# Moving the second half of the first v from SyncE's DMA queue to GpSimd's, with another share of rows for each DMA engine

## Chip, cores, metric

One core of a Trainium2 chip. The metric is the device time of one execution in microseconds (us).

## The reference

```python
# attn_weights: (8, 12, 1024, 1024) float32, v: (8, 12, 1024, 64) float32
def reference(attn_weights, v):
    return np.einsum('bhqs,bhsd->bhqd', attn_weights, v).astype(np.float32)
```

It reads 403 MB of weights and 25 MB of v and writes 25 MB (the page has 427.82 MB read and 25.17 MB written). Nearly all of the time is the reading of the weights: the last of them land at 1031.2 of 1052.7 us.

Of the kernel before, what the change touches and what calls it, by code (L numbers as in the profile page):

```python
# [10 lines left out]
def kernel(  # L11
# [18 lines left out]
    nc = tc.nc  # L30
    fp32 = mybir.dt.float32
# [6 lines left out]
    P = 128  # L38
# [17 lines left out]
    NO = 8 + 2  # L56
# [3 lines left out]
    def slot(q):  # L60
# [7 lines left out]
    v_2 = v.rearrange("b h q d -> (b h) q d").rearrange(  # L68
        "(hq two four) (p r) d -> hq (four p) two (r d)", two=2, four=VH, p=VP
    )  # L70
# [11 lines left out]
    with tc.tile_critical(no_gpsimd_drain=True):  # L82
        sem = tc.alloc_semaphore
        sb = lambda name, shape, dt: nc.alloc_sbuf_tensor(name, shape, dt).ap()
# [4 lines left out]
        vr = sb("vr", [P, 2, VB, SB * D], bf16)  # L89
        vbf = sb("vbf", [P, SB, VH, D], bf16)  # L90
        ot = sb("ot", [P, GH, P], fp32)
        osb = sb("osb", [P, NO, 2 * G, D], fp32)

        v32 = osb[:, ds(NO - 2, 2)].rearrange("p n r d -> p (n r d)")
        bank = [nc.alloc_psum_tensor(f"bank{i}", [P, 512], fp32).ap() for i in range(8)]
        pt = [b.rearrange("p (k j) -> p k j", k=KW) for b in bank[:4]]
        po = bank[4:6]
# [2 lines left out]

        s_abf = [sem(f"s_abf{i}") for i in range(2)]
        s_second = {n: sem(f"s_second{n}") for n in range(HALVED, NU)}
        s_v0, s_v = sem("s_v0"), sem("s_v")
        s_osb = [sem(f"s_osb{i}") for i in range(2)]
        s_held, s_end = sem("s_held"), sem("s_end")

# [11 lines left out]
        s_memset, s_const, s_vr = sem("s_memset"), sem("s_const"), sem("s_vr")  # L118
# [184 lines left out]

        for h in range(2):
            nc.vector.memset(ot[:, :, ds(h * HP, HP)], 0.0).then_inc(s_ot[h])
        nc.vector.wait_ge(s_v0, 16 * 4)
        nc.vector.tensor_copy(out=vr.rearrange("p two b x -> p (two b x)"), in_=v32).then_inc(s_vr, 2)  # L307
        engine(True)
        engine(False)

# [1 line left out]
        pool = nc.gpsimd  # L312

        def load_attn(n):
            pieces = [(0, G)] if n < HALVED else [(0, GH), (GH, GH)]
            for g0, gn in pieces:
                pool.dma_start(  # L317
                    out=abf[n % 2][:, ds(g0, gn)].rearrange("p g s -> p (g s)"),
                    in_=attn_q[n // 2][:, ds((n % 2 * G + g0) * S, gn * S)],
                ).then_inc(s_abf[n % 2] if g0 == 0 else s_second[n], 16)  # L320
# [15 lines left out]
        def store_2(q):  # L336
            store(q, 2, pool, s_osb[q // 2 % 2] if q < HELD_FROM else s_held)

        load_attn(0)
        load_attn(1)  # L340
        pool.wait_ge(s_memset, 2)
        pool.affine_select(
            out=ident,
            in_=ident,
# [7 lines left out]
        for h in range(VH):  # L352
            pool.wait_ge(s_const, h + 1)
            pool.affine_select(  # L354
                out=spread[ds(h * VP, VP)],
                in_=spread[ds(h * VP, VP)],
# [6 lines left out]
        for n in range(NU - 2):  # L363
            q, i = n // 2, n % 2
# [10 lines left out]
        pool.drain()  # L375





        v32_2 = v32.rearrange("p (two x) -> p two x", two=2)
        for two, p0, pn in ((0, 0, P), (1, 0, 96), (1, 96, 22), (1, 118, 10)):
            nc.sync.dma_start(
                out=v32_2[ds(p0, pn), two], in_=v_2[0][ds(p0, pn), two]
            ).then_inc(s_v0, 16)
        nc.sync.sem_inc(s_free, 2)
        for n in range(-2, NU - 2):

            if n + 2 < HALVED:
                nc.sync.wait_ge(s_abf[n % 2], 16 * ((n + 2) // 2 + 1))  # L390
            else:
                nc.sync.wait_ge(s_second[n + 2], 16)
            nc.sync.sem_inc(s_half)  # L393
            if n >= 0 and n % 2 == 0:
                q = n // 2
                if q % 2 == 1 and q + 1 < NV:
                    nc.sync.wait_ge(s_v, 16 * ((q + 1) // 2))
                    nc.sync.sem_inc(s_vr, 2)
                if q % 2 == 1 and 1 < q <= HELD_FROM:
                    nc.sync.wait_ge(s_osb[(q - 3) // 2 % 2], 16 * ((q - 3) // 4 + 1))  # L400
                    nc.sync.sem_inc(s_free)
# [10 lines left out]
        for k in range(2):  # L412
            nc.sync.wait_ge(s_osb[k], 16 * (HELD_FROM // 4))
        nc.sync.wait_ge(s_held, 16 * (BY_SYNC - HELD_FROM) // 2)
        nc.sync.wait_ge(s_end, 16 * 5)


# [28 lines left out]
```

## The kernel before: what the change touches

The weights come in 48 loads of 8 MB (64 KB in each of 128 rows; GpSimd's queue casts them to bf16 on the way, 4 MB land: 128 packets of 32768 bytes for each load in the trace). Two buffers take them in turn, and load n+2 is issued when PE has transposed load n. The v of eight heads comes as 128 rows of two halves; later v's come by GpSimd's queue too, but the first one comes by SyncE's queue, in float32, into a part of the output buffer that is not needed yet, and VectorE casts it:

```python
v32 = osb[:, ds(NO - 2, 2)].rearrange("p n r d -> p (n r d)")
...
# VectorE
nc.vector.wait_ge(s_v0, 16 * 4)
nc.vector.tensor_copy(out=vr.rearrange("p two b x -> p (two b x)"), in_=v32).then_inc(s_vr, 2)
...
# GpSimd
load_attn(0)
load_attn(1)
...                                     # constants
for n in range(NU - 2):                 # NU = 48
    q, i = n // 2, n % 2
    if i == 0 and q % 2 == 1 and q + 1 < NV:
        ...                             # wait until the v before is used
        load_v((q + 1) // 2)
    pool.wait_ge(s_t[True], (n + 1) * PER_DVE)
    load_attn(n + 2)
    if i == 0 and q % 2 == 0 and 0 < q <= HELD_FROM:
        store_2(q - 2)                  # 2 MB of the output, single_packet=True
...
# SyncE
v32_2 = v32.rearrange("p (two x) -> p two x", two=2)
for two, p0, pn in ((0, 0, P), (1, 0, 96), (1, 96, 22), (1, 118, 10)):
    nc.sync.dma_start(
        out=v32_2[ds(p0, pn), two], in_=v_2[0][ds(p0, pn), two]
    ).then_inc(s_v0, 16)
```

The split 96, 22 and 10 of the second half was already a balance: the rows per engine that the prediction counts in the trace, 17 on ten, 16 on one and 14 on five, fit eight rows of the first half and six of the 96 on each engine, two of the 22 rows on 11 engines and one of the 10 rows on ten of these, so that five engines get fewer rows.

## Time and profile before

| | before |
|---|---|
| median of the first three runs | 1055.8 us (1054.4 to 1056.23) |
| span in the profile | 1052.7 us |
| DMA engines' mean busy share | 90% or more in 39 of 40 slices, 80% to 90% in the last |
| PE, VectorE, ScalarE busy | 70%, 37%, 38% |
| last weights landed | 1031.2 us |

The waits say the same from two sides (columns: who waited for whom, us in total, times, longest us); the first line is from the view of all engines, the second from SyncE's queue:

```profile
POOL abf L317 <- PE bank L130: 689.1, 35, 34.0
...
SPq L393 <- DMA abf<-in_attn_weights_dram: 1025.5, 48, 25.7
```

GpSimd waits for PE before it may issue a load, which looks like a PE bound. But SyncE, which does little else than wait for loads to land, waits 1025.5 of 1052.7 us for them: there is always a load under way.

Besides the views, this document uses the trace's packet records: start, duration, size and queue of each DMA packet. They do not name the DMA engine; the prediction tells how packets were chained by time. That an engine sends one packet after the other is taken from the records: with 0.03 us taken off the end of each packet (a weight packet starts 0.02 us before the one ahead of it ends), more than 16 packets are under way at no time from 3 to 1030 us before. The 16 completion marks of each load are taken to tell when each engine was done with it: in load 2 before, each of its 16 packets of 4 bytes starts within 0.02 us of the end of a weight packet, at 65.30 to 67.07 us, and the marks come at 65.58 to 67.36 us. A number given to an engine here is a place in the layout of the rows; no record shows it. "The landing of load 2" below is the last of its 16 marks; loads count from 0.

Two packets of 16 KB come by an instruction queue (q8). Before, they start at 45.99 us (0.94 us long) and 56.29 us (0.98 us), and the weight packets right behind them take 2.605 and 2.607 us instead of 2.432, so each sets the engine that carries it back by 1.1 us.

### The profile page before, as it was taken

What the parts mean: (1) busy time and instruction counts of PE and PEld (TensorE: products, weight loads), DVE (VectorE), ACT (ScalarE), POOL (GpSimd) and SP (SyncE); (2) the same over time, 40 slices, a digit from 0 to 9 for tenths busy, and PEclk for the clock granted to TensorE, in tenths of its full rate; (3) what the DMA queues carried; (4) which work ended last, traced back from release to release, by engine and by line L of the source; (5) the groups of instructions that cost most, each with busy time, mean ns of one, the idle gap of its engine ahead of it and who ended that gap; (6) DMA issues with size and microseconds to landing.
All of it is one profiled execution on the core that took longest, in us unless ns stands there. A gap on an engine that the chain in (4) does not pass through costs nothing.

```text
span 1052.7 us, 16283 instructions
## 1 busy us (share of the span) xinstructions
PE 733.0 (70%) x6920; PEld 687.1 (65%) x6920; DVE 388.2 (37%) x582; ACT 397.8 (38%) x485; POOL 45.1 (4%) x80
## 2 busy tenths in 40 slices
PE   0777687676687567667768657775766865875885
PEld 0767676566687567656668557765666865865875
DVE  0543344333353234333335324433333433532543
ACT  0443344433353334333335324433333533533543
POOL 1000000000000000000000000000000000000000
PEclk9989888898798888889879878888887987988998
DMA  9999999999999999999999999999999999999998
GB/s 236 223 219 216 212 252 219 219 218 247 232 212 252 215 219 258 218 219 228 241 214 215 259 218 218 259 219 213 247 220 219 218 209 228 218 206 224 211 217 341
DMA packets 14332, 240.20 MB, mean 228 GB/s; under 512 B 1269, under 2 KB 1781, under 8 KB 4725
## 3 DMA queue, kind: packets, MB, share of 16 engines
q0 software_dynamic: 12912, 233.84, 99.1%
q1 hardware_dynamic: 1413, 6.29, 1.5%
q8 instruction: 2, 0.03, 0.0%
q14 instruction: 5, 0.04, 0.0%
HBM read 427.82 MB, written 25.17 MB: 430 GB/s over the span
## 4 chain that ended last, share of the span: by engine, by line
DMA 77%; PE 21%; issue 1%; POOL 0%; DVE 0%; ACT 0%; POOLq 0%; SPq 0%
DMA abf<-in_attn_weights_dram 77%; PE bank L130 20%; PE bank L172 0%; PE bank L157 0%; POOL abf L317 0%; DVE osb L237 0%; ACT ot L266 0%; POOLq L441 0%; SPq L393 0%; SPq L82 0%
## 5 line engine op out<-in xcount | busy, mean ns | idle before, releaser
L130 PE MATMUL bank<-ident,abf 128*128 128x128 f32 x3072 | 449.1, 316 | 278.0 <-DMA abf<-in_attn_weights_dram 272.6
L130 PEld LDWEIGHTS bank<-ident,abf 128*128 128x128 f32 x3072 | 439.2, 214 | 291.3 <-DMA abf<-in_attn_weights_dram 284.7
L254 DVE COPY at<-bank 128x1024 bf16<-128x1024 bf16 x480 | 319.8, 689 | 466.0 <-PE bank L130 463.0
L254 ACT COPY at<-bank 128x1024 bf16<-128x1024 bf16 x288 | 288.8, 1012 | 429.9 <-PE bank L130 429.9
L172 PE MATMUL bank<-at,vbf 128*64 128x256 bf16 x3072 | 215.0, 278 | 0.0
L172 PEld LDWEIGHTS bank<-at,vbf 128*64 128x64 bf16 x3072 | 196.8, 108 | 13.4 <-DVE at L254 4.0
L266 ACT COPY ot<-bank 128x512 f32<-128x512 f32 x48 | 28.1, 586 | 181.0 <-PE bank L172 181.0
L266 DVE COPY ot<-bank 128x512 f32<-128x512 f32 x48 | 33.2, 692 | 151.4 <-PE bank L172 151.4
L157 PE MATMUL bank<-ident,ot 128*128 128x128 f32 x392 | 52.2, 276 | 33.0 <-DVE vbf L230 32.2
L157 PEld LDWEIGHTS bank<-ident,ot 128*128 128x128 f32 x392 | 43.4, 141 | 45.0 <-DVE vbf L230 44.0
L237 ACT COPY osb<-bank 128x512 f32<-128x512 f32 x97 | 52.2, 589 | 22.5 <-PE bank L157 22.5
L317 POOL DMA_DIRECT2D abf<-in_attn_weights_dram x50 | 27.3, 546 | 690.2 <-PE bank L130 689.1
L230 DVE CAST vbf<-bank 128x512 bf16<-128x512 f32 x48 | 30.9, 686 | 6.5 <-PE bank L145 6.5
L230 ACT CAST vbf<-bank 128x512 bf16<-128x512 f32 x48 | 25.8, 589 | 11.9 <-PE bank L145 11.9
L145 PE MATMUL bank<-vr,spread 32*128 32x512 bf16 x384 | 25.7, 377 | 0.0
L323 POOL DMA_DIRECT2D vr<-in_v_dram x11 | 7.8, 706 | 238.5 <-PE bank L145 238.5
L145 PEld LDWEIGHTS bank<-vr,spread 32*128 32x128 bf16 x384 | 10.0, 92 | 6.9
L307 DVE CAST vr<-osb 128x4096 bf16<-128x4096 f32 x1 | 2.3, 2294 | 28.3 <-DMA osb<-in_v_dram 28.3
L330 POOL DMA_DIRECT2D out_dram<-osb x10 | 7.2, 717 | 28.6 <-ACT osb L237 28.6
L254 ACT ACT_TABLE_LOAD x4 | 5.1, 1283 | 1.1 <-SPq L82 1.1
L354 POOL TENSOR_SCALAR_AFFINE_SELECT spread<-spread 32x512 bf16<-32x512 bf16 x4 | 2.5, 632 | 0.6
L237 DVE COPY osb<-bank 128x512 f32<-128x512 f32 x1 | 0.7, 693 | 3.1 <-PE bank L157 3.1
(8 smaller groups left out, 2.1 us busy)
## 6 DMA issues: line engine op xcount, KB each, us to landing
abf<-in_attn_weights_dram POOLq DMA_DIRECT2D x46, 4096.0 KB, 33.4
out_dram<-osb POOLq DMA_DIRECT2D x10, 2048.0 KB, 29.5
vr<-in_v_dram POOLq DMA_DIRECT2D x11, 1024.0 KB, 17.4
abf<-in_attn_weights_dram POOLq DMA_DIRECT2D x4, 2048.0 KB, 24.2
out_dram<-osb SPq DMA_DIRECT2D x1, 2048.0 KB, 13.7
osb<-in_v_dram SPq DMA_DIRECT2D x1, 1024.0 KB
out_dram<-osb SPq DMA_DIRECT2D x1, 1024.0 KB, 16.0
osb<-in_v_dram SPq DMA_DIRECT2D x1, 768.0 KB
```

Source lines behind the costliest of these rows:

```text
L130: last = pe.matmul(out=pt[g % 4][:, k], lhsT=words[:, k], rhs=ident, is_transpose=True, start=(k == 0), stop=(k == KW - 1),)
L145: last = pe.matmul(out=ps, lhsT=spread[rows, b], rhs=vr[rows, two, b], start=(b == 0), stop=(b == VB - 1),)
L157: last = pe.matmul(out=ps[:, ds(j * P, P)], lhsT=ot[:, j0 + j], rhs=ident, is_transpose=True, start=(j == 0), stop=(j == jn - 1),)
L172: last = pe.matmul(out=outs, lhsT=vbf[:, 2 * kw + par, h], rhs=at[:, ds(half * GH, GH), kw, ds(h * VP, VP), par], start=(n == 0), stop=(n ...
L230: copy(out=vbf[:, :, h], in_=ps.rearrange("p (k d) -> p k d", k=SB)).then_inc(s_vbf[e])
L237: return copy(out=rows.rearrange("p (half j) d -> p j half d", half=2)[:, ds(j0, jn)], in_=ps[:, ds(0, jn * P)].rearrange("p (j half d) -> ...
L254: ins = copy(out=at[:, g].rearrange("c k j two -> c (k j two)"), in_=bank[g % 4].bitcast(bf16),)
L266: copy(out=ot.rearrange("c j (h p) -> c h j p", h=VH)[:, ds(2 * e, 2)], in_=po[e].rearrange("c (h j p) -> c h j p", h=2, j=GH),).then_inc( ...
L317: pool.dma_start(out=abf[n % 2][:, ds(g0, gn)].rearrange("p g s -> p (g s)"), in_=attn_q[n // 2][:, ds((n % 2 * G + g0) * S, gn * S)],).th ...
L323: pool.dma_start(out=vr.rearrange("p two b x -> p two (b x)"), in_=v_2[iv]).then_inc(s_v, 16)
L330: eng.dma_start(out=out_2[q // 2] if fours == 2 else out_q[q], in_=at_slot if fours == 2 else at_slot[:, 0], **({"single_packet": True} if ...
L354: pool.affine_select(out=spread[ds(h * VP, VP)], in_=spread[ds(h * VP, VP)], compare_op=mybir.AluOpType.not_equal, fill=1.0, base=0, patte ...
```

## The change

Its intent, read from the diff: only the first half stays on SyncE's queue; the second goes straight into its bf16 place by GpSimd's queue, behind loads 0 and 1. Three tiny transfers into an unused tile stand around the rows; the author took them to be there to shift which engines the 42 rows leave out.

```diff
-        v32 = osb[:, ds(NO - 2, 2)].rearrange("p n r d -> p (n r d)")
+        v32 = osb[:, NO - 1].rearrange("p r d -> p (r d)")
+        unused = sb("unused", [13, 3, 16], fp32)
...
-        nc.vector.wait_ge(s_v0, 16 * 4)
-        nc.vector.tensor_copy(out=vr.rearrange("p two b x -> p (two b x)"), in_=v32).then_inc(s_vr, 2)
+        nc.vector.wait_ge(s_v0, 16)
+        nc.vector.tensor_copy(out=vr[:, 0].rearrange("p b x -> p (b x)"), in_=v32).then_inc(s_vr)
...
+        to, of = vr[:, 1].rearrange("p b x -> p (b x)"), v_2[0][:, 1]
+        def lead(i, k):
+            pool.dma_start(out=unused[0:k, i], in_=v_2[0][0:k, 0, 0:16]).then_inc(s_unused, 16)
+        def rows_of_v(p0, p1):
+            pool.dma_start(out=to[p0:p1], in_=of[p0:p1]).then_inc(s_v1, 16)
+        lead(0, 13)
+        rows_of_v(0, 42)
+        lead(1, 5)
+        rows_of_v(42, 122)
+        rows_of_v(122, 128)
+        lead(2, 10)
...
-        for two, p0, pn in ((0, 0, P), (1, 0, 96), (1, 96, 22), (1, 118, 10)):
-            nc.sync.dma_start(...).then_inc(s_v0, 16)
+        nc.sync.dma_start(out=v32, in_=v_2[0][:, 0]).then_inc(s_v0, 16)
...
+            if n == 0:
+                nc.sync.wait_ge(s_v1, 16 * 3)
+                nc.sync.sem_inc(s_vr)
...
+        nc.sync.wait_ge(s_unused, 16 * 3)
```

More of the change, by code (lines that the diff above doesn't have):

```diff
@@ L102 @@
         s_second = {n: sem(f"s_second{n}") for n in range(HALVED, NU)}
-        s_v0, s_v = sem("s_v0"), sem("s_v")
+        s_v0, s_v1, s_v, s_unused = sem("s_v0"), sem("s_v1"), sem("s_v"), sem("s_unused")
         s_osb = [sem(f"s_osb{i}") for i in range(2)]
@@ L375 @@
         pool.drain()
-        v32_2 = v32.rearrange("p (two x) -> p two x", two=2)
-        for two, p0, pn in ((0, 0, P), (1, 0, 96), (1, 96, 22), (1, 118, 10)):
-            nc.sync.dma_start(
-                out=v32_2[ds(p0, pn), two], in_=v_2[0][ds(p0, pn), two]
-            ).then_inc(s_v0, 16)
+        nc.sync.dma_start(out=v32, in_=v_2[0][:, 0]).then_inc(s_v0, 16)
         nc.sync.sem_inc(s_free, 2)
         for n in range(-2, NU - 2):
+            if n == 0:
+                nc.sync.wait_ge(s_v1, 16 * 3)
+                nc.sync.sem_inc(s_vr)
             if n + 2 < HALVED:
```

## The prediction

Step 2 shared the rows among the engines: two engines, called 11 and 12, get five rows of the second half (six before), the others eight or nine; "11 to 15" are the five with the fewest rows before.

> **What bounds the kernel now.** I read the page first, then the chain of waits, then the timeline of the first 60 us, then the trace's records of single DMA packets. The page, parts 2 to 4:
>
> ```profile
> DMA  9999999999999999999999999999999999999998
> ...
> q0 software_dynamic: 12912, 233.84, 99.1%
> q1 hardware_dynamic: 1413, 6.29, 1.5%
> q8 instruction: 2, 0.03, 0.0%
> ...
> DMA 77%; PE 21%; issue 1%; POOL 0%; DVE 0%; ACT 0%; POOLq 0%; SPq 0%
> ```
>
> The 16 DMA engines are full in every slice; GpSimd's queue (q0) alone takes 99.1% of their time, SyncE's (q1) 1.5%. The chain's 21% on PE is not a PE bound, as its pieces show (start us, length us, what):
>
> ```profile
> 2.16 45.86 DMA abf<-in_attn_weights_dram
> 48.07 8.03 PE bank L130 x64
> 56.10 0.29 issue
> 56.39 30.33 DMA abf<-in_attn_weights_dram
> ...
> 1001.34 29.87 DMA abf<-in_attn_weights_dram
> 1031.29 5.60 PE bank L130 x32
> ```
>
> A load is issued when its buffer is free, but its packets then stand behind those of the load before it, so the eight microseconds of PE lie beside that load's packets. The bound is a sum of packet times on each DMA engine, from the first packet to the landing of the last attention weights at about 1031.2 us. The 21.5 us from there to the end (1052.7) are transposes, products and the last stores, which the change does not touch.
>
> The start, which the change does touch, in the timeline:
>
> ```profile
> 0.96 1.91 SPq L383 DMA_DIRECT2D osb<-in_v_dram  x4
> 1.48 1.24 POOL L317 DMA_DIRECT2D abf<-in_attn_weights_dram  x2 [1.04 <-SPq L82]
> 28.63 3.69 PE L130 MATMUL bank<-ident,abf 128*128 128x128 f32 x16 [28.63 <-DMA abf<-in_attn_weights_dram]
> 30.87 2.29 DVE L307 CAST vr<-osb 128x4096 bf16<-128x4096 f32 x1 [28.31 <-DMA osb<-in_v_dram]
> 33.82 6.08 PE L130 MATMUL bank<-ident,abf 128*128 128x128 f32 x48 [1.51 <-DVE at L254]
> 40.20 0.57 POOL L317 DMA_DIRECT2D abf<-in_attn_weights_dram  x1 [33.98 <-PE bank L130]
> ```
>
> The reader is to see that DVE waits 28.31 us for the first v, that its cast then holds PE for 1.51 us, and that load 2 goes out at 40.20 us, still before load 1 has landed (PE starts on it at 48.07).
>
> The packet records give start, duration, size and queue of each packet, not its engine; but an engine sends one after the other, so I chained them by time. What they show: a row of attention weights (64 KB read, 32 KB written) is one packet of 2.43 us, one every 2.41 us; a row of v takes 0.322 us by SyncE's queue and 0.324 us by GpSimd's, which casts it, one every 0.305 us. SyncE's first packets start at 1.98 us (eight engines) or 2.67 to 2.92 us (the other eight), GpSimd's first ones at 5.6 to 6.3 us on 14 engines and at 7.66 us on two. Two engines carry one 16 KB packet each of the instruction queue q8, at 45.99 us (0.94 us) and 56.29 us (0.98 us). From 3 us to 1030 us the engines' idle time is about 0.02 us in each 20 us.
>
> [...] the packets per chain at the start fit 17 rows on ten engines, 16 on one, 14 on five (they sum to 256), which is what 128, 96, 22 and 10 rows give. [...]
>
> **The change, part by part.**
> 1. Removed: 128 row packets on SyncE's queue. Added: 128 row packets on GpSimd's, behind loads 0 and 1. Mean per engine: 8 x 0.305 = 2.44 us taken out and put back. Sum zero. The f32 staging shrinks by half, which frees no time.
> 2. Added: three transfers of 13, 5 and 10 rows of 64 bytes into an unused tile, one or two small packets per engine. My estimate is at most 0.1 us on an engine (the trace's 4-byte packets take 0.02 us). [...]
> 3. What the new split is for: before, the three lightest chains that started early land load 1 at 46.00 to 46.31 us and the full ones at 46.9 to 47.35; then the q8 packet and the slower packet beside it set one engine back by 1.1 us, to 47.77 us, the last. An engine with 3.4 rows fewer (3.4 x 0.305 = 1.04 us) just absorbs such a packet: 8.4 rows against 5. So if 11 and 12 are the two that carry q8, all end load 1 and the v rows at about 5.9 + 16 x 2.41 + 8.5 x 0.305 = 47.1 us (estimate), up to 47.4 with the spread, and the last one gains about 0.4 us.
> 4. What it costs: SyncE's 8 rows are over at about 5.0 to 5.6 us and GpSimd's queue starts at 5.6 to 6.3. Before, second-half rows filled that gap; now it is idle: about 0.3 us on 14 engines. The two that start at 7.66 us are worse: before they moved some five rows of v meanwhile; now they idle about 2 us and owe those rows. If they are 11 and 12, they end at 7.66 + 38.6 + 5 x 0.305 = 47.8 us, or 48.9 with a q8 packet; if among 13 to 15, at 48.7 us. That is +0.1 to +1.1 us against 47.77. Their packet counts (about 14) put them among 11 to 15.
> 5. Off the path: the cast of v halves (2.29 us to an estimated 1.15 us) and need no longer wait for 28 us; load 0 lands without rows of v between its packets, so PE starts earlier by about 1.5 us and load 2 goes out perhaps 4 to 5 us earlier. Its queue is not empty at 40.20 us anyway, so this gives at most the 0 to 0.3 us by which the first engine runs dry near 46 us. The second half of v is in place at about 48 us and is used one loop round later, past 80 us.
>
> And the start is not all kept: the spread of the loads' landings falls from 1.77 us to 1.27 at about 148 us, where the last packets before the first store take 2.9 to 3.3 us on the leading engines. After that 13 engines lie within 0.8 us, and two trail, to 1.69 and 2.02 us at the end. An imbalance at the start is worth about half its size at the end. Sum: -0.4 + 0.3 to +1.1, halved: about -0.2 to +0.4 us. With the mark that whoever chose 42 rows and five rows for two engines will have aimed at the trailing ones, I take -0.2 us: 1055.8 to 1055.6.
>
> **The rivals.**
> First, the trailing engines at the end are exactly 11 and 12, and the row less there (6 to 5), with the load moved to engines that lead, shortens the end by 0.3 to 1 us: 1054.8 to 1055.5. For it: the clean arithmetic of 3.4 rows. Against: the two late starters, which lose their filling.
> Second, the late starters become the last ones and stay so: +1 us, 1056.8. For it: the gap of 1.5 us in the first GpSimd packets; against: the evening out at 148 us, and that the late start may itself come from SyncE's rows, which take 0.45 to 0.61 us instead of 0.32 on those two engines just then.
> Third, the early end of load 0 shortens the whole by several us because PE waits for 28.63 us at the start. Against: PE is never the bound later, the queues are full; worth nothing.
> Fourth, more packets on GpSimd's queue delay its descriptors for later loads. Load 2 is the first issued after them, at over 35 us, and six issues of about 0.55 to 0.7 us each are long over: 0 us.
>
> **Range and chances.** All of these lie within 2 us, 0.2% of the time. The three runs before spread over 1.8 us (1054.4 to 1056.23)[...], so the range that should hold the time 8 times in 10 is 1054.0 to 1057.4 us. For 2% (21 us) about ten rows of weights per engine would have to vanish or be added: faster 0.005, within 2% 0.985, slower 0.01 (a queue stall that I don't see).
>
> **What would show each step.** q1's bytes fall by 1 MB; q0 has 128 more packets of 4096 bytes and a few of 64. The cast of v is about 1.1 us long and comes before 10 us; PE starts at about 27 us and load 2 is issued at about 35 us. GpSimd's first packets start at the same 5.6 to 7.7 us; if those two engines are no longer late, step 4 is too dark. The landings of the last load show who trails: a spread clearly under 2.0 us with an earlier last one says the rebalancing works; about 3 us says rival two. The last landing should stay within 1 us of 1031.2 us and the tail at 21.5 us. I would be wrong if the tail, the load period of 43.5 us for two loads, or the idle time between 60 and 1000 us changed.

## The result, and the profile after

| | before | changed |
|---|---|---|
| median of 6 runs each | 1054.72 us (1054.37 to 1056.23) | 1055.17 us (1054.93 to 1055.92) |
| ratio | | 1.0003, 95% interval 0.999 to 1.0015 |

A ratio here is the mean time of one kernel's runs over that of the other's runs of the same rounds, so it is not quite the ratio of the medians quoted.

The timeline of the start (start us, busy us, engine, line, what, and in brackets the idle time before it and who ended it; line numbers are one or more higher than before):

```profile
0.96 0.39 SPq L397 DMA_DIRECT2D osb<-in_v_dram  x1
...
5.78 1.23 DVE L308 CAST vr<-osb 128x2048 bf16<-128x2048 f32 x1 [3.21 <-DMA osb<-in_v_dram]
...
25.08 10.33 PE L131 MATMUL bank<-ident,abf 128*128 128x128 f32 x64 [25.08 <-DMA abf<-in_attn_weights_dram]
...
35.71 0.59 POOL L318 DMA_DIRECT2D abf<-in_attn_weights_dram  x1 [25.47 <-PE bank L131]
```

The cast takes 1.23 us and is over at 7 us instead of 33. PE starts at 25.08 instead of 28.63 us and is not held up, and load 2 is issued at 35.71 instead of 40.20 us. The queues in the page:

```profile
q0 software_dynamic: 13200, 234.36, 99.4%
q1 hardware_dynamic: 1248, 5.24, 1.3%
q8 instruction: 2, 0.03, 0.0%
```

1 MB has left q1; q0's share rises from 99.1% to 99.4%, q1's falls from 1.5% to 1.3%. The work has changed queues and has not become less. The chain's last part:

```profile
1002.95 28.42 DMA abf<-in_attn_weights_dram
...
1031.45 6.69 PE bank L131 x32
```

PE starts on the last weights at 1031.45 us, 0.16 later than before, although it started on the first ones 3.55 us earlier.

The packet records show where the 3.55 us went. In the table "mean" is the mean of the 16 completion marks, "last" the last of them, and "stretched" is the time that weight packets took above their usual 2.432 us in the stretch from 144 to 151 us, summed over the engines:

| us | before | changed |
|---|---|---|
| GpSimd's first weight packets | 5.62 to 7.67 | 5.03 to 5.37 |
| load 0, last | 28.58 | 25.03 |
| load 2, mean / last | 66.55 / 67.36 | 66.21 / 67.14 |
| load at 130 us, mean / last | 129.44 / 130.22 | 129.10 / 130.01 |
| stretched | 5.0 | 14.7 |
| load at 150 us, mean / last | 149.10 / 149.92 | 149.36 / 150.48 |
| last load, mean / last | 1029.89 / 1031.21 | 1030.02 / 1031.37 |

Load 0 is early because rows of v no longer stand between its packets. Before, they came one between two rows of weights: most of them started at 8.08 to 8.70, 10.81 to 11.43 and 13.54 us and so on, 2.73 us apart (2.41 + 0.32), the last at 27.43 us. In the changed kernel the rows come after load 1, at 43.75 to 47.18 us, and by load 2 nothing of the 3.55 us is left but a mean lead of 0.34 us. The last engine leads by 0.22 us only. At 145 us both are lost in a stretch of slow packets, on the last weight rows ahead of the first store. The sum closes: from load 2 to the end the mean lead of 0.34 us turned into a lag of 0.13, a loss of 0.47 us, and the weight packets after 67 us were over their usual time by 9.1 us in sum before and 16.3 us in the changed kernel, which is 0.45 us per engine.

### The profile page after: what moved, and what is told of

Same layout as the page of the kernel before. It is cut to its first block, busy times and chain, and to the rows that moved or that the text cites. A ratio compares the mean times of both kernels' runs of the same rounds, so it can differ in the third digit from the quotient of the medians.

```text
span 1052.8 us, 16286 instructions
## 1 busy us (share of the span) xinstructions
PE 738.6 (70%) x6920; PEld 693.1 (66%) x6920; DVE 387.9 (37%) x582; ACT 397.7 (38%) x485; POOL 49.1 (5%) x86
## 3 DMA queue, kind: packets, MB, share of 16 engines
q0 software_dynamic: 13200, 234.36, 99.4%
## 4 chain that ended last, share of the span: by engine, by line
DMA 77%; PE 21%; issue 1%; POOL 0%; DVE 0%; ACT 0%; SPq 0%; POOLq 0%
DMA abf<-in_attn_weights_dram 77%; PE bank L131 20%; PE bank L173 0%; PE bank L158 0%; POOL abf L318 0%; DVE osb L238 0%; ACT ot L267 0%; POOLq L457 0%; SPq L408 0%; SPq L82 0%
## 5 line engine op out<-in xcount | busy, mean ns | idle before, releaser
L131 PE MATMUL bank<-ident,abf 128*128 128x128 f32 x3072 | 454.7, 319 | 273.7 <-DMA abf<-in_attn_weights_dram 269.7
L131 PEld LDWEIGHTS bank<-ident,abf 128*128 128x128 f32 x3072 | 445.2, 214 | 286.5 <-DMA abf<-in_attn_weights_dram 281.8
```

The lines of the kernel that those rows point to most:

```text
L131: last = pe.matmul(out=pt[g % 4][:, k], lhsT=words[:, k], rhs=ident, is_transpose=True, start=(k == 0), stop=(k == KW - 1),)
```

## The experiments

Twelve runs were made: the two kernels unchanged, nine other versions, and one of these a second time. My theory A: the end is a sum of packet times on each engine, so moving v gives nothing, and the uneven shares of rows matter only for the engine that trails. Two things stood against the intent of the change and had to be tested: whether the two engines with five rows are those that carry the instruction packets, and whether a start lead survives at all.

All runs (last landings in us, from the traces; the median of the kernel before is that of the same session; stretched as above, for the last two kernels with later stores at 164 to 168 us; "no second half" was read from 142.9 us):

| run | load 2, last | stretched | last of all | median | before | ratio |
|---|---|---|---|---|---|---|
| before again | 69.05 | 9.8 | 1032.27 | 1055.70 | 1054.94 | 1.0005 |
| changed again | 67.31 | 14.3 | 1031.93 | 1055.70 | 1054.94 | 1.0008 |
| plain | 67.23 | 10.9 | 1031.41 | 1055.15 | 1054.94 | 1.0003 |
| split as before | 66.66 | 11.5 | 1032.20 | 1055.56 | 1054.94 | 1.0006 |
| no second half | 64.69 | 10.9 | 1028.97 | 1052.76 | 1055.50 | 0.9975 |
| second half twice | 69.55 | 9.7 | 1033.78 | 1057.76 | 1055.50 | 1.0022 |
| no small transfers | 67.23 | 11.0 | 1032.19 | 1055.72 | 1055.50 | 1.0002 |
| no single packets | 67.16 | 10.9 | 1031.60 | 1055.47 | 1055.50 | 1.0002 |
| one SyncE transfer | 67.53 | 3.3 | 1031.68 | 1055.36 (one look) | 1055.37 | none |
| stores later | 67.39 | 14.0 | 1031.49 | 1055.08 | 1055.37 | 0.9996 |
| split again | 66.77 | 10.2 | 1032.15 | 1055.46 | 1055.37 | 0.9999 |
| split, stores later | 66.60 | 10.1 | 1030.65 | 1054.85 | 1055.27 | 1.0000 |

The 95% intervals of the ratios reach about 0.0015 to each side; only those of "no second half" (0.9962 to 0.9989) and "second half twice" (1.0009 to 1.0036) leave 1 out. So differences of under a microsecond between the other versions are read from the traces, one or two each, and not from the times.

### Both kernels once more

No edit.

> The kernel before, unchanged, for a second trace of it. Every theory expects the same time (ratio 1.000 within 0.1%). What it tells: how much the packet records repeat. If the landings of load 2 come again with the last at 67.1 to 67.4 us and 1.8 us of spread, and the two 16 KB instruction packets near 46 and 56 us hit the same kind of engine, the start is set by the program; if the one-off stretching of the packets near 145 to 150 us (5 us summed over the engines in the first trace) comes out otherwise, that part is chance.

> The changed kernel, unchanged. Ratio to the kernel before 0.999 to 1.001. Theory A (the shares of GpSimd's partial copies go from the lowest engine up, 42 rows as 3 on each of 14 engines, so the relief of 42 rows went to two engines that carry no instruction packet): the trace again has two engines that start load 2 near 45.6 us and one at 47.5 us with the first instruction packet, and the last landing of load 2 at about 67.1 us. Rival B [...]: in another execution the two relieved engines may be the ones with the instruction packets, and the last landing of load 2 falls to about 66.5 us. The stretching near 145 to 150 us (14.7 us summed in the first trace) repeats if it belongs to the kernel, and differs if it is chance.

The kernel before does not repeat at the start. In its second trace GpSimd's queue began on all engines at 5.8 to 6.3 us, so the two late engines at 7.66 us of the first trace did not come again. Otherwise its start came out worse. The chain of waits of this second trace:

```profile
2.34 30.55 DMA osb<-in_v_dram
...
35.94 8.07 PE bank L130 x48
```

Here the first v itself is on the chain, for 30.55 us; load 2 was issued at 44.31 us (40.20 in the first trace), and one engine ended load 2 at 69.05 us. The packet records show why that one: its first packet of load 2, at 47.67 us, took 4.13 us instead of 2.43. From 40 to 52 us weight packets were over their usual time by 5.5 us in sum, against 0.2 us in the first trace. Whether the late issue of load 2 slowed them, no run tests. The 16 KB instruction packets came on other engines, at 51.7 and 61.2 us (45.99 and 56.29 us in the first trace).

The changed kernel does repeat: load 2 landed at 67.14 and 67.31 us, with two engines that start load 2 early, near 45.7 us, and one late, at 47.5 and 47.7 us; the stretched packets sum to 14.7 and 14.3 us. So rival B, shares that differ from run to run, found no support. What the change did bring is a start with more room: load 2's packets stand ready some ten microseconds before they are wanted (issued at 35.71 us, the first one sent at 45.63 us), instead of two to six.

### One plain transfer of the second half

```diff
-        lead(0, 13)
-        rows_of_v(0, 42)
-        lead(1, 5)
-        rows_of_v(42, 122)
-        rows_of_v(122, 128)
-        lead(2, 10)
+        rows_of_v(0, 128)
```

> The second half of the first v as one GpSimd transfer of 128 rows, 8 on each engine, without the three small transfers. Theory A: the engines with the instruction packets carry 8 rows here as in the changed kernel, so the last landing of load 2 is the same, 67.1 us within 0.1, although every other engine differs; the time is that of the changed kernel within 0.1%. Rival C (the fine split is worth its 0.3 us of mean): it is 0.3 to 0.6 us longer than the changed kernel.

The last landing of load 2 is 67.23 us, as theory A said, and the median, 1055.15 us, is not longer than the changed kernel's 1055.70 us in the same session, so rival C falls. The starts of load 2 on the 16 engines, in us:

```
changed          45.63 45.66 | 46.26 46.28 46.29 46.35 46.38 46.40 46.43 | 46.81 46.82 46.86 46.86 46.87 46.88 | 47.53
no small ones    45.71 45.79 | 46.34 46.37 46.37 46.40 46.53 46.58 46.65 | 46.76 46.79 46.84 46.87 46.88 46.88 | 47.59
plain            46.26 to 46.57 on 15 engines                                                                  | 47.62
split as before  45.88 45.95 45.97 46.04 | 46.43 | 46.72 to 46.98 on 10 engines | 47.01
```

In the first three the last engine is the one with the first instruction packet and 8 rows of v. Taking six engines to 9 rows and two to 5 leaves it where it was.

### Without the small transfers

```diff
-        lead(0, 13)
         rows_of_v(0, 42)
-        lead(1, 5)
         rows_of_v(42, 122)
         rows_of_v(122, 128)
-        lead(2, 10)
```

> The changed kernel without its three small transfers: 42, 80 and 6 rows remain. Theory A (partial copies are laid from the lowest engine up, 3 rows each on 14 engines): the small transfers turn nothing, so again two engines start load 2 near 45.6 us with 5 rows, six have 9 rows and one is at 47.5 us with the instruction packet; same time within 0.1%. [...]

The second line of the table above: two engines with 5 rows, seven and one with 8, six with 9, exactly as with them. The small transfers shift nothing. The records of the changed kernel say how the rows are laid. The ten packets of the third small transfer come on the six engines that had just sent a ninth row and on four others, and not on the two with 5 rows; the five packets of the second one (44.90 to 44.97 us) come on engines that had just sent three of the 42 rows. None of these came on the two that the 42 rows had left out. The counts fit if every transfer begins on the same engine: 42 rows as 3 each on the first 14, 6 rows on the first 6, 5 on the first 5, 10 on the first 10. Then the two spared engines are the last two, 14 and 15. The first instruction packet sits on an engine that carries a packet of the first small transfer (engines 0 to 12), 8 rows, and none of the third (so not 0 to 9). That is 10, 11 or 12. The second one comes at 56.05 us, at the end of a packet of the engine that had started load 2 at 46.40 us, again one with 8 rows and no packet of the third (10 to 13). The next experiment narrows it: there both instruction packets sit on engines with 6 rows, which in this layout are 11 to 15 (the first on the one that starts load 2 at 47.01 us, the second, at 55.53 us, four packets after the start at 45.88 us). If the packets keep their engines from kernel to kernel, the first is on 11 or 12 and the second on 11, 12 or 13. So 11 and 12 may well be the right engines to spare; the change spared 14 and 15.

### The old split on the new queue

```diff
-        lead(0, 13)
-        rows_of_v(0, 42)
-        lead(1, 5)
-        rows_of_v(42, 122)
-        rows_of_v(122, 128)
-        lead(2, 10)
+        rows_of_v(0, 96)
+        rows_of_v(96, 118)
+        rows_of_v(118, 128)
```

> GpSimd's queue as in the change, but the rows split as the kernel before had them: 96, 22 and 10 rows, which by theory A gives 9 rows on engines 0 to 9, 8 on 10 and 6 on 11 to 15. If the two engines with the instruction packets are among 11 to 15, they carry two rows less than in the changed kernel: the last landing of load 2 falls from 67.14 us by 2 x 0.305 = 0.6 us to about 66.5 us, and the last landing of all by 0.3 to 0.6 us; time about 0.5 us under the changed kernel (ratio to the kernel before 0.9993 to 1.0000). [...]

> The split of the kernel before (96, 22 and 10 rows) by GpSimd's queue once more, with more rounds. Theory A with chance later on: the last landing of load 2 is again near 66.6 us, 0.5 us ahead of the changed kernel, but where the last landing of all comes (1030.6 to 1032.3 us) depends on stretched packets that differ from run to run; the ratio to the kernel before stays within 0.999 to 1.001. Rival: the first run's late engine was an exception, and the version is 0.5 us faster than the kernel before in the median.

At the start it does what theory A said. The engine with the first instruction packet now has 6 rows and starts load 2 at 47.01 us, level with the engines of 9 rows (last line of the fence above); load 2 lands at 66.66 and 66.77 us, 0.4 to 0.7 us ahead of the changed kernel. But the last landing of all is 1032.20 and 1032.15 us, later than in both traces of the changed kernel. In between, in the first of these traces, weight packets are stretched by 2.3 us in sum at 320 us, 0.7 at 495, 1.8 at 583 and 1.0 at 670, and from 480 us on the trailing engine falls from 1.4 to 2.7 us behind the first; in the second, by 3.2 at 495 and 4.1 at 669. Those times differ from trace to trace in size, not in place: they are 87 us apart, one for each store. My expectation of 0.5 us less time was a miss; that of the second run, "within 0.999 to 1.001", held.

### Does a row at the start reach the end?

Eight rows fewer on each engine (wrong result: the first half is used twice), and eight rows more:

```diff
# no second half: VectorE copies the first half into both places; no second transfer
+        nc.vector.tensor_copy(out=vr[:, 1].rearrange("p b x -> p (b x)"), in_=v32).then_inc(s_vr)
# second half twice
+        rows_of_v(0, 128)
+        pool.dma_start(out=unused, in_=of).then_inc(s_unused, 16)
```

> A wrong result on purpose: the second half of the first v is not transferred; VectorE copies the first half twice. That takes 8 row packets (8 x 0.305 = 2.44 us) from every DMA engine and leaves the rest. Theory A (the end is a sum of packets per engine): all landings come 2.4 us earlier, the last one of load 2 at about 64.7 us, the time falls by about 2.4 us (ratio to the kernel before 0.9975 to 0.998). Rival D (the start is made good later anyway, by waits at the stores): the time falls by under 1 us.

> The plain GpSimd transfer of the second half, and the same rows once more into an unused tile: 8 row packets (2.44 us) more on every engine. Theory A: 2.4 us longer than the plain one (ratio to the kernel before 1.0023 to 1.003). Rival D: under 1 us longer.

The chain of the kernel without the second half, and then that of the kernel with it twice:

```profile
999.10 29.87 DMA abf<-in_attn_weights_dram
1029.05 5.59 PE bank L131 x32
```

```profile
1005.36 28.41 DMA abf<-in_attn_weights_dram
1033.85 5.33 PE bank L131 x32
```

Against the plain kernel's last landing of 1031.41 us that is 2.44 us earlier (1028.97) and 2.37 us later (1033.78); 8 rows at 0.305 us are 2.44. The last landing alone can differ by half a microsecond or more between two traces of one kernel, so the closeness is partly luck; the means of the 16 last landings say the same, 2.36 us earlier and 2.38 us later. A row that is on all engines reaches the end in full, in the times too: ratios 0.9975 and 1.0022 (the second just under the expected 1.0023). So rival D falls, and so does the thought that uniform work at the start is hidden.

The records of all 14 traces go further. Take the mean of the 16 last landings, subtract the mean landing of load 2, and subtract a sixteenth of all the time by which weight packets after 67 us were over 2.432 us: what is left is 962.76 to 962.83 us in every trace. So what an engine has at load 2 is kept in the mean, and what comes later is only the stretched packets. They do not even out the engines as a rule: over the first store, the distance from the first to the last of the 16 landings fell from 1.75 to 1.25 us in the first trace of the kernel before, but rose from 1.31 to 2.33 us in the plain kernel and from 1.91 to 2.01 us in the changed one.

### What stretches the packets before a store?

First, the form of the store:

```diff
-                **({"single_packet": True} if eng is pool else {}),
```

> The changed kernel with GpSimd's stores no longer asked for as single packets. It asks what stretches the last weight packets before the first store (14.7 and 14.3 us summed over the engines in two traces of the changed kernel, at 144.7 to 150 us). If it is the single-packet form of the store, the stretch sums fall to near 0 and the last landing comes 0.5 us or more earlier, unless the stores themselves get slower; if it is any store's first packets, the sums stay above 5 us. Time: same within 0.1% either way.

10.9 us are stretched at the first store and 3.8 us at the second: asking for single packets is not the cause. The records show the same 2560 packets of 8 KB, of 0.309 us each in the middle, with and without the request, so they do not tell whether it changed the transfer at all. Then the place of the store, one load later:

```diff
-            if i == 0 and q % 2 == 0 and 0 < q <= HELD_FROM:
+            if i == 1 and q % 2 == 0 and 0 < q <= HELD_FROM:
                 store_2(q - 2)
```

> The changed kernel with GpSimd's stores issued one load later (behind the next load). In all ten traces so far the one large stretching of weight packets sits on the last row of the load ahead of the first store (about 143 to 150 us). Theory E (it belongs to the change from weights to stores in the queue): it moves with the store by one load, to about 165 to 172 us. Rival F (it belongs to a point of time or to an address): it stays at 143 to 150 us. Time within 0.1% of the changed kernel.

Theory E held. The stretching moved to 164 to 168 us (14.0 us) and none is left at 145. PE's waits show it without packet records. First the timeline of PE in the changed kernel, then in this one (the number in brackets is PE's wait for the load):

```profile
130.05 8.02 PE L131 MATMUL bank<-ident,abf 128*128 128x128 f32 x64 [1.29 <-DMA abf<-in_attn_weights_dram]
150.53 1.77 PE L131 MATMUL bank<-ident,abf 128*128 128x128 f32 x7 [7.17 <-DMA abf<-in_attn_weights_dram]
```

```profile
130.30 8.02 PE L131 MATMUL bank<-ident,abf 128*128 128x128 f32 x64 [1.25 <-DMA abf<-in_attn_weights_dram]
149.62 2.62 PE L131 MATMUL bank<-ident,abf 128*128 128x128 f32 x11 [6.03 <-DMA abf<-in_attn_weights_dram]
```

From one start to the next it is 20.48 us in the changed kernel and 19.32 us here: the load between has lost its slow packets. At the old later places (233, 320, 407 us) no packet was over its time by more than 0.023 us in this trace; at the moved ones, a load later (252, 339, 426 us), by no more than 0.07 us. The time: 1055.08 us, ratio 0.9996. What in the step from weights to stores slows the packets, and why the first store is by far the worst, stays open: I moved it and did not take it away. Open too is whether the change itself makes it larger: the three traces with all of the first v on SyncE's queue have 3.3, 5.0 and 9.8 us, the eleven others 9.7 to 14.7 us, and no experiment separates that from chance.

### One SyncE transfer for all of v

```diff
-        nc.vector.wait_ge(s_v0, 16 * 4)
+        nc.vector.wait_ge(s_v0, 16)
...
-        for two, p0, pn in ((0, 0, P), (1, 0, 96), (1, 96, 22), (1, 118, 10)):
-            nc.sync.dma_start(
-                out=v32_2[ds(p0, pn), two], in_=v_2[0][ds(p0, pn), two]
-            ).then_inc(s_v0, 16)
+        nc.sync.dma_start(out=v32_2, in_=v_2[0]).then_inc(s_v0, 16)
```

> The kernel before with its four SyncE transfers of the first v made one, 16 rows on each engine. In two traces of the kernel before GpSimd's first weight packets start at 5.6 to 7.7 and 5.8 to 6.3 us, in the kernels with one SyncE transfer at 4.9 to 5.5 us. If the number of SyncE transfers is the cause, they start at 5.0 to 5.5 us here too; if the rows of SyncE's queue that stand ready are the cause, at 5.6 us and later. The engines with the instruction packets carry 8 rows of the second half, two more than before: the last landing of load 2 at 67.4 to 68 us. Time within 0.1% of the kernel before.

GpSimd's first weight packets start at 5.59 to 6.26 us, as with four transfers. So it is the rows that stand ready in SyncE's queue, not the number of its transfers. In the first trace of the kernel before, with 14 to 17 rows for each engine there, the engines sent 166 rows before their first weight packets, 10.4 on the mean, and began on the weights at 5.62 to 7.67 us; in the changed kernel, with eight each, they sent all 128 and began at 5.03 to 5.37 us. Why the rows did not alternate with weights from the start, as they did from 8 us on, these runs do not show. Nor do they show whether GpSimd's packets could have begun earlier than 5.0 us.

### Both helpful parts together

The split 96, 22, 10 and the later stores; the edits are those above.

> The two helpful parts together: GpSimd's queue with the split 96, 22 and 10, and the stores one load later. The split brought the last landing of load 2 to 66.7 and 66.8 us (67.1 to 67.4 in the changed kernel); the later stores left no weight packet of the loads at 233, 320 and 407 us stretched by more than 0.02 us in their one trace. If both hold, the last landing of all comes at 1030.5 to 1031.0 us and the time is 0.5 to 1 us under the kernel before (ratio 0.999 to 0.9996), which is still inside the verdict same. Rival: the absence of later stretching was chance; then the last landing is anywhere from 1031.2 to 1032.3 us and the ratio 0.9995 to 1.0005.

The chain of its last part, to hold against 1031.45 us of the changed kernel:

```profile
1000.54 30.11 DMA abf<-in_attn_weights_dram
...
1030.72 5.59 PE bank L131 x32
```

The last landing, 1030.65 us, is the earliest of all complete versions, and the span, 1052.2 us, the shortest. The times are not better by anything that can be told: median 1054.85 us against 1055.27, but a mean ratio of 1.0000 (interval 0.9987 to 1.0014), because one of five runs took 1055.96 us. It beats neither kernel.

## Why the prediction was right, point by point

The predicted 1055.6 us met 1055.17, and "within 2%" was never in doubt. The forecast gain of 0.2 us was not tested: the kernel before, taken as 1055.8 us from three runs, has a median of 1054.72 us in six, and the measured difference of the means, +0.27 us, has an interval from -1.1 to +1.6 us. Nor did it come from the working: -0.4 plus 0.3 to 1.1, halved, is -0.05 to +0.35 us and not -0.2 to +0.4, and the -0.2 was chosen for the supposed intent of the change. The parts fared less evenly.

- **Bound and sum zero (step 1): right.** Eight rows less or more on each engine moved the last landing by -2.44 and +2.37 us; the change moved eight rows from one queue to the other and added none.
- **The shares (step 2): the counts were right, the engines wrong.** The counts, 9, 8 and 5 rows on six, eight and two engines, are those of the trace. The spared engines are the last two in the layout that fits, and the small transfers shift nothing: without them the starts of load 2 fall into the same groups (two near 45.7 us, six from 46.76 to 46.88 us).
- **The gain of up to 0.4 us (step 3): wrong as to who gets it.** The arithmetic that 3.4 rows pay for one instruction packet held: with two rows fewer the engine that carries it started load 2 at 47.01 instead of 47.53 us, and if the five rows had come on it, it would have started at about 46.6 us (estimate: 47.53 less 3 x 0.305), so that the engines with nine rows, at 46.88 us, would have been the last. As the rows were laid, it had 8 rows, two more than before, and kept the last place. The last landing of load 2 improved by 0.22 us.
- **The idle gap and the two late starters (step 4): wrong, and by luck on the other side.** There was no gap: GpSimd's packets began (5.03 to 5.37 us) the moment SyncE's eight rows were through (5.03 to 5.37 us). The late starters came in only one trace of the kernel before. The mean gained 0.34 us where I had booked a loss of 0.3.
- **Off the path (step 5): right in what it costs, with the start of PE mis-sized.** The cast took 1.23 us (estimated 1.15), load 2 was issued at 35.71 us (estimated about 35). PE started at 25.08 us, 3.55 us earlier than before and not 1.5.
- **"Worth half at the end": wrong as a rule.** The prediction saw the step at the first store in one trace and took it for an evening out. A uniform row was kept in full; and of the twelve traces with the store at its old place, the distance between the first and the last engine fell over the store by more than 0.2 us in four and rose by more than 0.4 us in four. In the profiled run the stretching took the whole lead of 0.34 us and 0.26 more, because it was 14.7 us in sum against 5.0. In the second trace of the kernel before it was 9.8: part of the difference may be chance.
- The rivals: that the early end of load 0 is worth nothing held. The rival with late starters as the last ones fell with the late starters. That the added issues delay no later load held too: the six were over at 5.78 us, and load 2 was issued at 35.71 us.
- The tail from the last landing to the end was 21.45 us (21.5 predicted).

## What to carry to other kernels

Here the DMA engines were full (90% or more in 39 of 40 slices), and moving 128 rows of v from one queue to the other changed when things land (load 0 by 3.55 us) and not how long the whole takes (the last landing by 0.16 us); in such a case look for the mean over all engines and for the engine that trails, not for the first landing. Balancing shares by single rows (0.3 us each) is only worth it when the stretches that come later are smaller (here 3.3 to 14.7 us over 16 engines at the first store), and one trace cannot tell: here the last landing came at 1031.37 and 1031.93 us in two executions of the changed kernel. Before steering rows to chosen engines, check in the packet records of a run which engines got them.
